# A decoder block on one core: 208 instead of 192 tokens take the gathered path of the expert layer, with other buffers and another order of its routing

## The chip, the cores and the metric

The kernel runs on one core of one Trainium2 chip. The metric is the time of one execution on the device in microseconds (us). The kernel before took 3613.26 us (median of three runs, 3609.4 to 3621.5).

## The reference, cut to what matters

512 tokens of width 2048, all in float32. A norm and one projection give the inputs of two mixers, a short convolution and a stick-breaking attention; both are gated, summed, projected and added to x. Then comes the expert layer:

```
q      = xn @ wq                                # 8 heads x 2 x 128
scores = q . subkeys                            # two lists of 128 a head
top 16 of each list; 256 sums; top 16 of them   # 16 of 16384 experts a head
gate   = softmax(the 16 scores)
hidden = xn . u[idx]                            # 8 x 16 = 128 experts a token
out    = sum(gelu(hidden) * gate * v[idx])
x      = rmsnorm(x + out)
```

u and v have 16384 rows of 2048. Each token uses 128 of them.

## The kernel before, in words

**Two ways through the expert layer.** The first G0 = 192 tokens are *gathered*: for each of a token's 128 experts the row of u, and later of v, is fetched from memory. One round fetches one row for each of 128 partitions (an indirect transfer of 1 MB issued by POOL, L690); VectorE (DVE) multiplies it with the token's xn and sums (L701, table u), or adds it, scaled, to a sum (L708, table v). A tile of 128 tokens takes 128 rounds of u and 128 of v. The next 64 tokens lie twice in the 128 partitions, with half of the slots each, and take 64 + 64. At the end of a tile `finish` folds the copies, and `finish_rows` takes the last norm and stores. The other ND = 320 tokens go the *dense* way (`dense`): all 16384 experts are computed for them and multiplied by a matrix of gates that is zero nearly everywhere.

**Weights.** `whalf` loads 128x1024 numbers (0.5 MB) by an SP transfer into a raw tile, and `split` makes two float32r parts: ScalarE (ACT) writes whi (L130), DVE writes wlo (L131). `mm3` does three matmuls with them (L161 to L163), whose moving operand is the tokens: 256 columns in the mixers and queries, 320 in the dense stage. There are WHL = 3 pairs whi/wlo, and 4 raw tiles `wraw`. In the dense stage every second half goes to one of three `spare` tiles instead.

**Stages.** First token half: mixer, output projection, queries (until about 805 us). Second half: mixer (`ahead`, to 1480), output projection, queries (to 1706). Then `dense`: eight chunks of `up` (u products, 8 units each), then per chunk `down` (v products), and from the ninth chunk on `up` and `down` in turn. A unit is two halves of weights, 48 matmuls; the dense stage has 256.

**What runs beside.** Two generators are advanced by hand between the units. `side` is routing: per tile of 128 tokens the top 16 lists (`top16`), the sums, one-hot selections, and the indices and gates; later `gates` turns the gates of the dense tokens into planes, in NB = 20 blocks of 16 tokens, four groups each. Every yield of it names a cost, and `background` grants 1.0 to 1.25 a call. `gat` is the gather; `pump(rate)` grants rounds per unit (1.35, then 0.85 and 0.8; 1.0 in the second queries and early dense stage; behind the routing the rest is spread evenly, at 0.9 of the even rate in the first eight chunks). A fetch also waits for an anchor, an instruction two units back (`LAG`), and a row is consumed one round after its fetch (`DEPTH`); L701 and L708 keep their program order. The tile framework then orders each engine's instructions by a simulated timeline, so loads are often issued earlier than they stand in the program. The `row` tiles are four, shared by the gather, the attention and the loads of rows.

Of the kernel before, what the change touches and what calls it, by code (L numbers as in the profile page):

```python
# [18 lines left out]
P = 128  # L19
# [6 lines left out]
H = 8  # L26
# [5 lines left out]
NG2 = 64  # L32
# [30 lines left out]
SPB2 = 3  # L63
# [13 lines left out]
AHEAD = 8  # L77


@with_exitstack  # L80
def block_kernel(ctx, tc, a, out, dbg=None):
# [104 lines left out]
    def rms_scale(pool, x):  # L186
        ss = pool.tile([P, 2], F32, name="ss", bufs=2)
        for c in range(2):
            junk = ztile()
            nc.scalar.activation(junk, x[:, c * 1024:c * 1024 + 1024], AF.Square, accum_out=ss[:, c:c + 1])  # L190
        return rms_inv(ss)

    def rms_inv(ss):
        nc.vector.tensor_tensor(ss[:, 0:1], ss[:, 0:1], ss[:, 1:2], OP.add)
        nc.scalar.activation(ss[:, 0:1], ss[:, 0:1], AF.Sqrt, scale=1.0 / D, bias=epst)
        nc.vector.reciprocal(ss[:, 0:1], ss[:, 0:1])
        return ss[:, 0:1]
# [356 lines left out]
    def route(pool, tile_no, st):  # L554

        ls = pool.tile([P, 2, 8, 2, 16], F32, name="ls", bufs=1)
        tv, ti = ls[:, 0], ls[:, 1].bitcast(U32)
        for _ in range(8):
            while not st["topk"][tile_no]:
                yield "wait"  # L560
            for _ in range(2):
                src, g = st["topk"][tile_no].pop(0)
                tmp = pool.tile([P, P], F32, name="ttmp", bufs=2)
                top16(tmp, src, tv[:, g // 2, g % 2], ti[:, g // 2, g % 2])
            yield 2.0
        tif = pool.tile([P, 8, 2, 16], F32, name="tif", bufs=1)
# [3 lines left out]
        cand = spare()[:, 0:512].rearrange("p (h c) -> p h c", h=8)  # L570
        c0 = 0
        for a0, na, nb in GROUPS:
            nc.vector.tensor_tensor(cand[:, :, c0:c0 + na * nb].rearrange("p h (a b) -> p h a b", b=nb),
                                    tv[:, :, 0, a0:a0 + na].unsqueeze(3).broadcast_to([P, 8, na, nb]),
                                    tv[:, :, 1, 0:nb].unsqueeze(2).broadcast_to([P, 8, na, nb]), OP.add)
            c0 += na * nb
        yield 0.9
        sv = pool.tile([P, 8, 16], F32, name="sv", bufs=1)
        pos = pool.tile([P, 8, 16], U32, name="pos", bufs=1)
        for h in range(H):  # L580
            tmp = pool.tile([P, P], F32, name="ttmp", bufs=2)
            top16(tmp[:, 0:64], cand[:, h], sv[:, h], pos[:, h])
            if h % 2:
                yield 1.4
        eg = pool.tile([P, 3, 8, 16], F32, name="eg", bufs=2)

        ic = pool.tile([P, 2, 8, 16], U32, name="ic", bufs=1)
# [3 lines left out]
        fa = pool.tile([P, 8, 16], F32, name="fa", bufs=1)  # L591
        fb = pool.tile([P, 8, 16], F32, name="fb", bufs=1)
        f1 = pool.tile([P, 8, 16], F32, name="f1", bufs=1)
        f2 = pool.tile([P, 8, 16], F32, name="f2", bufs=1)
# [13 lines left out]
        yield 2.6  # L608
        for s, ab in enumerate((fa, fb)):
            for h in range(0, H, 4):  # L610
                oh = spare().rearrange("p (h s k) -> p h s k", h=4, s=16)
                nc.vector.tensor_tensor(oh, ab[:, h:h + 4].unsqueeze(3).broadcast_to([P, 4, 16, 16]),
                                        iota[:, 0:16].unsqueeze(1).unsqueeze(1).broadcast_to([P, 4, 16, 16]), OP.is_equal)
                nc.vector.tensor_tensor(oh, oh, tif[:, h:h + 4, s].unsqueeze(2).broadcast_to([P, 4, 16, 16]), OP.mult)
                nc.vector.tensor_reduce(eg[:, s, h:h + 4], oh, AX.X, OP.add)
                yield 3.5
        gate = eg[:, 2]
        nc.vector.tensor_tensor(gate, sv, sv[:, :, 0:1].broadcast_to([P, 8, 16]), OP.subtract)
        nc.scalar.activation(gate, gate, AF.Exp)
        gs = pool.tile([P, 8], F32, name="gs", bufs=1)  # L620
        nc.vector.tensor_reduce(gs, gate, AX.X, OP.add)
        nc.vector.reciprocal(gs, gs)
        nc.vector.tensor_tensor(gate, gate, gs.unsqueeze(2).broadcast_to([P, 8, 16]), OP.mult)
        flat = eg.rearrange("p s a b -> p s (a b)")
        idx = None
        if tile_no * P < G0:
            ef = pool.tile([P, P], F32, name="fa", bufs=1)
            nc.vector.scalar_tensor_tensor(ef, flat[:, 0], 128.0, flat[:, 1], OP.mult, OP.add)
            idx = late[1].tile([P, P], I32, name="idx", bufs=2)
            nc.vector.tensor_copy(idx, ef)  # L630
            if tile_no == 0:
                st["gate"] = late[1].tile([P, P], F32, name="gate", bufs=1)
                nc.vector.tensor_copy(st["gate"], flat[:, 2])
        if dbg:
            nc.sync.dma_start(dbg["eg"][tile_no], flat)
        st["routes"][tile_no] = idx, flat
        yield 1.2
# [43 lines left out]
    def gather_tile(pool, np_, nslot, idx, gate, load_x, load_acc, finish):  # L681
# [6 lines left out]
        def fetch(tab, s):  # L688
            g = row()[0:np_]
            ins = nc.gpsimd.indirect_dma_start(out=g, out_offset=None, in_=tab, in_offset=bass.IndirectOffsetOnAxis(ap=idx[0:np_, s:s + 1], axis=0))  # L690
# [4 lines left out]
        acc = None  # L695

        def consume(tab, s, g):
            nonlocal acc
# [4 lines left out]
            if s == 0:  # L703
                nc.scalar.activation(act[:, :nslot], hid[:, :nslot], AF.Gelu)
                nc.vector.tensor_tensor(act[:, :nslot], act[:, :nslot], gate[0:np_], OP.mult)
                acc = row()
                load_acc(acc)
            pin(nc.vector.scalar_tensor_tensor(acc[0:np_], g, act[:, s:s + 1], acc[0:np_], OP.mult, OP.add))  # L708

        ready = []  # L710
        for tab in ("u", "v"):
            for s in range(nslot):
                ready.append((tab, s, fetch(a[tab], s)))
                if len(ready) > DEPTH:
                    consume(*ready.pop(0))
                yield
        while ready:
            consume(*ready.pop(0))
            yield
        finish(acc)  # L720
# [12 lines left out]
    def gather(routes):  # L733
        idx = routes[0][0]
        yield from gather_tile(
            late[1], P, P, idx, st["gate"],
            lambda t: nc.sync.dma_start(t, xn2d[0:P]),
            lambda t: nc.sync.dma_start(t, x2d[0:P]),
            lambda t: finish_rows(t, slice(0, P), final_gain()))
        if not NG2:  # L740
            return
        S = P // (P // NG2)
        idx, eg = routes[1]
        idx2 = late[1].tile([P, S], I32, name="idx2")
        gate2 = late[1].tile([P, S], F32, name="gate2")
        for r in range(P // NG2):
            ps_, ss = slice(r * NG2, r * NG2 + NG2), slice(r * S, r * S + S)
            nc.sync.dma_start(idx2[ps_], idx[0:NG2, ss])
            nc.sync.dma_start(gate2[ps_], eg[0:NG2, 2, ss])

        def load_x(t):
            for r in range(P // NG2):
                nc.sync.dma_start(t[r * NG2:r * NG2 + NG2], xn2d[P:G0])

        def load_acc(t):
            nc.vector.memset(t, 0.0)
            nc.sync.dma_start(t[0:NG2], x2d[P:G0])

        def finish(t):
            for r in range(1, P // NG2):  # L760
                o = row()
                nc.sync.dma_start(o[0:NG2], t[r * NG2:r * NG2 + NG2])
                nc.vector.tensor_tensor(t[0:NG2], t[0:NG2], o[0:NG2], OP.add)
            finish_rows(t, slice(P, G0), final_gain())

        yield from gather_tile(late[1], P // NG2 * NG2, S, idx2, gate2, load_x, load_acc, finish)

# [136 lines left out]
    st = {"routes": [None] * 4}  # L904
# [4 lines left out]
    rounds = 2 * P + (2 * (P // (P // NG2)) if NG2 else 0)  # L909
# [9 lines left out]
    def routing(h):  # L919
        for tt in range(2):  # L920
            yield from route(rts[0], 2 * h + tt, st)
# [43 lines left out]
    def background(what, rate):  # L965
# [3 lines left out]
        due = min(due, 0.0) + (SIDE_A0 if not st["routes"][0] else SIDE_A if unit < GATES_AT else SIDE_G)  # L969
# [11 lines left out]
        if st["routes"][0] and what != "half":  # L981
# [115 lines left out]
```

## Time and profile before

| | |
|---|---|
| median of three runs | 3613.26 us |
| the profiled execution | 3619.12 us, span 3617.4 us |
| granted TensorE clock, mean | 0.992 |
| PE, PEld busy | 3513.1 us (97%), 3410.4 us (94%) |
| DVE, ACT, POOL busy | 2831.2 us (78%), 1616.3 us (45%), 659.3 us (18%) |
| moved by DMA | 1049.29 MB, of which indirect 402.68 MB |
| rounds of the gather | 192 of u, 192 of v |

PE is TensorE's matmuls, PEld its weight loads, which overlap them. The clock is a share of full speed. A wait is named "who line <- whom", with its sum, its count and the longest. The chain is the work that ended last, followed back from the end.

### The profile page before, as it was taken

Reading aid. Unit: us, or ns where it says so; the run is one execution under the profiler, and the core shown is the slowest. Engines: PE = TensorE matmul, PEld = TensorE weight load, DVE = VectorE, ACT = ScalarE, POOL = GpSimd, SP = SyncE. Lnnn points to the kernel's source line nnn. Section 1 sums busy time; section 2 is a strip of 40 time slices with the busy share of each in tenths; the row PEclk is TensorE's granted clock in tenths of the full one; section 3 lists DMA queues with packets and bytes.
Section 4 is the critical chain, followed back from the end, with each engine's and each line's share of the span. In section 5 each row is a group of like instructions: output and inputs, shape, how many; then the busy total and the mean of one; then the engine's idle time right before and its main releaser. Section 6 shows DMA issues by size and latency. Waiting matters only on the chain.

```text
span 3617.4 us, 63262 instructions
## 1 busy us (share of the span) xinstructions
PE 3513.1 (97%) x25347; PEld 3410.4 (94%) x25347; DVE 2831.2 (78%) x4022; ACT 1616.3 (45%) x2275; POOL 659.3 (18%) x520
## 2 busy tenths in 40 slices
PE   9999999999999999889999999999999999999998
PEld 8999998898888999779999999999999999999998
DVE  6565557559987878788999886888887878888886
ACT  6454445445555534544337773333333333333334
POOL 0000000001233322112131111221122322322220
PEclk9999999999999999999999999999999999999999
DMA  6556555654788889898888889899988988899884
GB/s 204 180 178 225 187 187 196 208 184 137 260 348 309 335 332 346 322 331 335 298 327 319 311 315 365 329 356 338 339 328 328 346 330 333 327 346 343 328 329 162
DMA packets 292920, 1049.29 MB, mean 290 GB/s; under 512 B 35921, under 2 KB 105169, under 8 KB 238673
## 3 DMA queue, kind: packets, MB, share of 16 engines
q1 hardware_dynamic: 237328, 642.56, 50.5%
q0 software_dynamic: 55296, 402.68, 28.7%
q8 instruction: 199, 3.26, 0.4%
q14 instruction: 97, 0.79, 0.1%
HBM read 996.57 MB, written 47.97 MB: 289 GB/s over the span
## 4 chain that ended last, share of the span: by engine, by line
PE 59%; DMA 5%; DVE 4%; issue 2%; ACT 1%; POOL 0%; SPq 0%; ACTq 0%; DVEq 0%; POOLq 0%
PE pj L163 10%; PE pj L161 10%; PE pj L162 10%; PE z L161 9%; PE z L162 9%; PE z L163 9%; DVE wlo L131 2%; DMA wraw<-in_w_in 2%; PE pj L673 2%; DMA row<-in_u,idx 1%; DVE row L701 1%; ACT whi L130 1%; PE z L439 1%; DMA row<-in_v,idx 0%; DMA wraw<-in_w_mix 0%
## 5 line engine op out<-in xcount | busy, mean ns | idle before, releaser
L130 ACT ACTIVATE whi<-wraw 128x1024 fp32r<-128x1024 f32 x827 | 874.1, 1059 | 1258.0 <-PE pj L162 723.2
L131 DVE TENSOR_TENSOR wlo<-wraw,whi 128x1024 fp32r<-128x1024 f32 x827 | 1008.3, 1223 | 412.5 <-ACT whi L130 405.6
L161 PE MATMUL pj<-xhi,whi 128*128 128x256 f32 x2560 | 723.5, 283 | 12.5 <-ACT whi L130 10.3
L163 PE MATMUL pj<-xhi,wlo 128*128 128x256 f32 x2560 | 720.4, 283 | 13.5 <-DVE wlo L131 13.4
L162 PE MATMUL pj<-xlo,whi 128*128 128x256 f32 x2560 | 718.1, 281 | 0.0
L161 PE MATMUL pj<-dxhi,whi 128*128 128x320 f32 (+1 forms) x2304 | 710.0, 308 | 4.5 <-ACT whi L130 4.3
L163 PE MATMUL pj<-dxhi,wlo 128*128 128x320 f32 (+1 forms) x2304 | 703.6, 307 | 3.4 <-DVE wlo L131 3.3
L162 PE MATMUL pj<-dxlo,whi 128*128 128x320 f32 (+1 forms) x2304 | 705.2, 306 | 0.0
L161 PE MATMUL z<-ahi,whi 128*128 128x320 f32 x2048 | 632.0, 310 | 3.9 <-ACT z L190 2.9
L162 PE MATMUL z<-alo,whi 128*128 128x320 f32 x2048 | 631.8, 309 | 2.4 <-DVE alo L131 2.4
L163 PE MATMUL z<-ahi,wlo 128*128 128x320 f32 x2048 | 630.6, 309 | 1.8 <-DVE wlo L131 1.8
L163 PEld LDWEIGHTS pj<-xhi,wlo 128*128 128x128 f32 x2560 | 481.6, 189 | 23.6 <-DVE wlo L131 20.9
L161 PEld LDWEIGHTS pj<-xhi,whi 128*128 128x128 f32 x2560 | 482.5, 188 | 21.1 <-ACT whi L130 14.4
L690 POOL DMA_INDIRECT row<-in_v,idx x192 | 292.7, 1525 | 1060.2 <-DVE row L708 429.8
L162 PEld LDWEIGHTS pj<-xlo,whi 128*128 128x128 f32 x2560 | 482.3, 188 | 2.8 <-issue 1.6
L708 DVE SCALAR_TENSOR_TENSOR row<-row,gact 128x2048 f32<-128x2048 f32 x192 | 450.3, 2345 | 27.2 <-DMA row<-in_v,idx 27.2
L701 DVE SCALAR_TENSOR_TENSOR row<-row,gx 128x2048 f32<-128x2048 f32 x192 | 438.3, 2286 | 31.2 <-DMA row<-in_u,idx 31.1
L690 POOL DMA_INDIRECT row<-in_u,idx x192 | 289.0, 1505 | 863.1 <-DVE row L701 239.9
L161 PEld LDWEIGHTS pj<-dxhi,whi 128*128 128x128 f32 x2304 | 434.3, 189 | 5.5 <-ACT whi L130 5.1
L163 PEld LDWEIGHTS pj<-dxhi,wlo 128*128 128x128 f32 x2304 | 432.9, 188 | 5.4 <-DVE wlo L131 5.4
L162 PEld LDWEIGHTS pj<-dxlo,whi 128*128 128x128 f32 x2304 | 434.0, 188 | 0.0
L130 ACT ACTIVATE whi<-spare 128x1024 fp32r<-128x1024 f32 x197 | 208.8, 1060 | 425.4 <-PE z L162 266.9
(232 smaller groups left out, 4979.8 us busy)
## 6 DMA issues: line engine op xcount, KB each, us to landing
wraw<-in_w_in SPq DMA_DIRECT2D x320, 512.0 KB
wraw<-in_uT SPq DMA_DIRECT2D x187, 512.0 KB
wraw<-in_vT SPq DMA_DIRECT2D x128, 512.0 KB
spare<-in_vT SPq DMA_DIRECT2D x128, 512.0 KB
spare<-in_uT SPq DMA_DIRECT2D x69, 512.0 KB
wraw<-in_w_mix SPq DMA_DIRECT2D x64, 512.0 KB
wraw<-in_w_out SPq DMA_DIRECT2D x64, 512.0 KB
wraw<-in_wq SPq DMA_DIRECT2D x64, 512.0 KB
```

What stands on the lines that cost most here:

```text
L130: nc.scalar.activation(hi, src, AF.Copy)
L131: nc.vector.tensor_tensor(lo, src, hi.bitcast(F32), OP.subtract)
L161: nc.tensor.matmul(acc, shi, mhi, start=first, stop=False)
L162: nc.tensor.matmul(acc, shi, mlo, start=False, stop=False)
L163: pe_last[0] = nc.tensor.matmul(acc, slo, mhi, start=False, stop=last)
L439: nc.tensor.matmul(z[:, c], stat.bitcast(F32), src[:, c], start=False, stop=True, skip_group_check=True)
L673: behind(nc.tensor.matmul(gp[:, t * P:t * P + P], oh[:, t, 0], oh[:, t, 1], start=True, stop=True))
L690: ins = nc.gpsimd.indirect_dma_start(out=g, out_offset=None, in_=tab, in_offset=bass.IndirectOffsetOnAxis(ap=idx[0:np_, s:s + 1], axis=0))
L701: pin(nc.vector.scalar_tensor_tensor(g, g, 1.0, gx, OP.mult, OP.mult, accum_out=hid[:, s:s + 1]))
L708: pin(nc.vector.scalar_tensor_tensor(acc[0:np_], g, act[:, s:s + 1], acc[0:np_], OP.mult, OP.add))
```

## The change

Before, tile 0 (128 tokens) and 64 tokens of tile 1 are gathered. Now a list of segments does it: 128 tokens, 64 (two copies), and 16 (eight copies, folded three times). 208 + 208 rounds. The dense stage keeps 304 tokens (19 gate blocks).

In the dense stage there is one `spare` tile, used by every fifth half, and a fourth whi/wlo pair, used by every fourth. The routing works on half a tile's heads at a time. The first four heads of tile 0 are done as soon as their scores exist, and the gather starts on their indices; tile 1's lists are made between, and the rest of its routing follows with all costs times four (`LATE_W`). The v sum goes into gx, the tile that held xn; x2d is loaded and added at the end of a segment. The square sums of `rms_scale` go through a small tile of SBUF, 256 columns at a time.

```diff
+SEGS = ((0, 0, 128), (1, 0, 64), (1, 64, 16))
-NG2 = 64
+NG2 = 80
-SPB2 = 3
+SPB2 = 1
+LATE_W = 4.0
 def whalf(src):
-        if spare_ok[0] and turns[0] % 2:
+        if spare_ok[0] and turns[0] % 5 == 0:
             raw = spare()
...
-        hi = wp.tile([P, 1024], F32R, name="whi", bufs=WHL)
-        lo = wp.tile([P, 1024], F32R, name="wlo", bufs=WHL)
+        if spare_ok[0] and turns[0] % (WHL + 1) == 0:
+            hi, lo = (late[2].tile([P, 1024], F32R, name=n, bufs=1) for n in ("whi4", "wlo4"))
+        else:
+            hi, lo = (wp.tile([P, 1024], F32R, name=n, bufs=WHL) for n in ("whi", "wlo"))
 def rms_scale(pool, x):
-        for c in range(2):
-            junk = ztile()
+        for c in range(8):
+            junk = pool.tile([P, 256], F32, name="junk", bufs=1)
...
 def route_lists(pool, tile_no, hh, st):          # new: lists of heads 4*hh to 4*hh+3
 def route(pool, tile_no, hh, st, w):             # the rest for these heads, costs times w
...
+            idx = late[1].tile([P, 64], I32, name=f"idx_{hh}", bufs=2)
+            nc.vector.tensor_copy(idx, ef)
+            st["idx"][tile_no].append(idx)
 def gather_tile(...):
...
-                acc = row()
-                load_acc(acc)
-            pin(nc.vector.scalar_tensor_tensor(acc[0:np_], g, act[:, s:s + 1], acc[0:np_], OP.mult, OP.add))
+                pin(nc.vector.tensor_scalar(gx, g, act[:, 0:1], None, OP.mult))
+                return
+            pin(nc.vector.scalar_tensor_tensor(g if s == nslot - 1 else gx, g, act[:, s:s + 1], gx, OP.mult, OP.add))
...
+                while s // idx[0].shape[1] >= len(idx):
+                    yield
 def gather(routes):
+        for tile_no, p0, n in SEGS:
...
+            def finish(t):
+                m = P // 2
+                while m >= n:
+                    o = row()
+                    nc.sync.dma_start(o[0:m], t[m:2 * m])
+                    nc.vector.tensor_tensor(t[0:m], t[0:m], o[0:m], OP.add)
+                    m //= 2
+                o = row()
+                nc.sync.dma_start(o[0:n], x2d[rows])
+                nc.vector.tensor_tensor(t[0:n], t[0:n], o[0:n], OP.add)
+                finish_rows(t, rows, final_gain())
 def routing(h):
-        for tt in range(2):
-            yield from route(rts[0], 2 * h + tt, st)
+        for hh in range(2):
+            yield from route_lists(rts[0], ta, hh, st)
+            yield from route(rts[0], ta, hh, st, 1.0)
+            if h:
+                yield from route_lists(rts[0], tb, hh, st)
+                yield from route(rts[0], tb, hh, st, 1.0)
+            else:
+                yield from route_lists(rts[0], tb, hh, st)
+                kept.append(st["ls"][tb])
+        for hh, ls in enumerate(kept):
+            st["ls"][tb] = ls
+            yield from route(rts[0], tb, hh, st, LATE_W)
 def background(what, rate):
-        due = min(due, 0.0) + (SIDE_A0 if not st["routes"][0] else SIDE_A if unit < GATES_AT else SIDE_G)
+        due = min(due, 0.0) + (SIDE_A0 if not st["idx"][0] else SIDE_A if unit < GATES_AT else SIDE_G)
...
-        if st["routes"][0] and what != "half":
+        if st["idx"][0] and what != "half":
```

## Rows read from the trace of the kernel before

**Rows 1.** The page: the span, and PE's busy time.

```profile
span 3617.4 us, 63262 instructions
PE 3513.1 (97%) x25347; PEld 3410.4 (94%) x25347; DVE 2831.2 (78%) x4022; ACT 1616.3 (45%) x2275; POOL 659.3 (18%) x520
```

**Rows 2.** Windows: length; PE, PEld, DVE, ACT, POOL busy; clock; DMA; GB/s.

```profile
740.00:805.00 65.00, 65.00 (x556) 65.00 (x555) 35.63 (x86) 26.80 (x33) 0.00 (x0) 1.00 0.52 172
805.00:905.00 100.00, 95.24 (x703) 84.12 (x701) 90.71 (x328) 55.08 (x65) 12.96 (x17) 1.00 0.43 142
905.00:1050.00 145.00, 136.70 (x1003) 121.21 (x1002) 133.73 (x249) 78.18 (x93) 49.87 (x45) 1.00 0.79 294
1050.00:1480.00 430.00, 399.03 (x3152) 378.10 (x3150) 341.70 (x376) 194.00 (x238) 116.01 (x92) 0.98 0.89 333
1706.00:2180.00 474.00, 468.70 (x3297) 465.88 (x3297) 426.55 (x966) 272.30 (x508) 85.74 (x58) 1.00 0.87 314
1800.00:1900.00 100.00, 99.38 (x676) 98.85 (x675) 98.40 (x197) 37.35 (x45) 29.12 (x13) 1.00 0.89 322
2215.00:2660.00 445.00, 439.82 (x2981) 436.93 (x2980) 381.57 (x365) 156.81 (x186) 89.71 (x63) 1.00 0.92 342
2400.00:2500.00 100.00, 99.08 (x673) 98.30 (x672) 86.88 (x85) 34.36 (x40) 21.71 (x16) 1.00 0.94 353
2660.00:3550.00 890.00, 887.11 (x6025) 886.16 (x6025) 725.98 (x657) 320.28 (x393) 228.39 (x140) 1.00 0.88 332
```

**Rows 3.** Windows with PE never idle, at 256 columns and at 320.

```profile
400.00:500.00 100.00, 100.00 (x851) 100.00 (x850) 57.72 (x72) 42.86 (x53) 0.00 (x0) 1.00 0.56 185
2860.00:3360.00 500.00, 500.00 (x3409) 499.75 (x3409) 411.39 (x382) 173.95 (x210) 140.61 (x83) 1.00 0.89 337
```

**Rows 4.** Timeline of ACT: start, duration, instruction, idle before and its releaser.

```profile
3001.84 1.06 ACT L130 ACTIVATE whi<-wraw 128x1024 fp32r<-128x1024 f32 x1 [2.46 <-PE z L162]
3005.36 1.06 ACT L130 ACTIVATE whi<-spare 128x1024 fp32r<-128x1024 f32 x1 [2.46 <-PE z L162]
```

**Rows 5.** Waits: span (four rows), DVE from 2260 to 3520, PE in 1000:1100.

```profile
POOL row L690 <- DVE row L708: 429.8, 88, 13.3
POOL row L690 <- DVE row L701: 247.2, 42, 25.3
DVE row L701 <- DMA row<-in_u,idx: 31.1, 24, 5.0
DVE hb L779 <- DMA gt<-gd: 8.7, 1, 8.7
...
DVE row L701 <- DMA row<-in_u,idx: 0.9, 2, 0.6
...
PE pj L163 <- DVE wlo L131: 6.7, 9, 1.2
```

**Rows 6.** Chain of waits: start, us, what; a gate group, a plane, a finish.

```profile
1499.85 0.89 PE pj L673 x8
...
2185.14 15.56 DMA gt<-gd
...
2747.74 1.16 ACT z L190 x2
```

**Rows 7.** Windows, columns as in rows 2: the plane's load, the first finish.

```profile
2180.00:2240.00 60.00, 56.14 (x364) 55.21 (x363) 37.23 (x38) 20.82 (x30) 11.37 (x7) 0.94 1.03 394
2740.00:2760.00 20.00, 17.14 (x99) 16.87 (x98) 14.63 (x15) 9.47 (x14) 2.77 (x2) 0.83 0.93 341
```

**Rows 8.** Windows of L690 alone (us, POOL busy); L701 and L753 by tile.

```profile
2180.00:2740.00 560.00, 114.02 (x79) 0.99 0.92 343
2740.00:3550.00 810.00, 210.95 (x128) 1.00 0.88 333
...
L701 DVE SCALAR_TENSOR_TENSOR row<-row,gx x192: 2241/2284/2486, 908.6 to 3147.6; 128x2048 f32<-128x2048 f32 x192
L753 SPq DMA_DIRECT2D gx<-xn2d x2: 480/534/588, 1797.2 to 1797.7; - x2
```

More of the change, by code (lines that the diff above doesn't have):

```diff
@@ L552, in top16, with route_lists @@
         nc.vector.max_index(ti[:, 8:16], tv[:, 8:16], tmp)
-    def route(pool, tile_no, st):
-        ls = pool.tile([P, 2, 8, 2, 16], F32, name="ls", bufs=1)
+    def route_lists(pool, tile_no, hh, st):
+        ls = st["ls"][tile_no] = pool.tile([P, 2, 4, 2, 16], F32, name="ls", bufs=3)
         tv, ti = ls[:, 0], ls[:, 1].bitcast(U32)
-        for _ in range(8):
+        for _ in range(4):
             while not st["topk"][tile_no]:
@@ L573, in route @@
             nc.vector.tensor_tensor(cand[:, :, c0:c0 + na * nb].rearrange("p h (a b) -> p h a b", b=nb),
-                                    tv[:, :, 0, a0:a0 + na].unsqueeze(3).broadcast_to([P, 8, na, nb]),
-                                    tv[:, :, 1, 0:nb].unsqueeze(2).broadcast_to([P, 8, na, nb]), OP.add)
+                                    tv[:, :, 0, a0:a0 + na].unsqueeze(3).broadcast_to([P, 4, na, nb]),
+                                    tv[:, :, 1, 0:nb].unsqueeze(2).broadcast_to([P, 4, na, nb]), OP.add)
             c0 += na * nb
[L577 to L580, printed above, removed]
+        yield 0.5 * w
+        sv = pool.tile([P, 4, 16], F32, name="sv", bufs=1)
+        pos = pool.tile([P, 4, 16], U32, name="pos", bufs=1)
+        for h in range(4):
             tmp = pool.tile([P, P], F32, name="ttmp", bufs=2)
@@ L607, in route @@
         nc.vector.tensor_tensor(fb, fb, f1, OP.add)
-        yield 2.6
+        yield 1.8 * w
         for s, ab in enumerate((fa, fb)):
[L610 to L616, printed above, removed]
@@ new lines, in route @@
+            nc.vector.tensor_reduce(eg[:, s, hs], oh, AX.X, OP.add)
+            yield 3.5 * w
+        flat = eg.rearrange("p s a b -> p s (a b)")
+        fs = slice(64 * hh, 64 * hh + 64)
+        if tile_no * P < G0:
+            ef = pool.tile([P, 64], F32, name="fa", bufs=1)
+            nc.vector.scalar_tensor_tensor(ef, flat[:, 0, fs], 128.0, flat[:, 1, fs], OP.mult, OP.add)
+            idx = late[1].tile([P, 64], I32, name=f"idx_{hh}", bufs=2)
+            nc.vector.tensor_copy(idx, ef)
+            st["idx"][tile_no].append(idx)
@@ L619, in route @@
+        gate = eg[:, 2, hs]
+        nc.vector.tensor_tensor(gate, sv, sv[:, :, 0:1].broadcast_to([P, 4, 16]), OP.subtract)
         nc.scalar.activation(gate, gate, AF.Exp)
-        gs = pool.tile([P, 8], F32, name="gs", bufs=1)
+        gs = pool.tile([P, 4], F32, name="gs", bufs=1)
         nc.vector.tensor_reduce(gs, gate, AX.X, OP.add)
         nc.vector.reciprocal(gs, gs)
-        nc.vector.tensor_tensor(gate, gate, gs.unsqueeze(2).broadcast_to([P, 8, 16]), OP.mult)
-        flat = eg.rearrange("p s a b -> p s (a b)")
@@ L636, in route @@
-        st["routes"][tile_no] = idx, flat
-        yield 1.2
+        nc.vector.tensor_tensor(gate, gate, gs.unsqueeze(2).broadcast_to([P, 4, 16]), OP.mult)
+        if tile_no == 0:
+            if hh == 0:
+                st["gate"] = late[1].tile([P, P], F32, name="gate", bufs=1)
+            nc.vector.tensor_copy(st["gate"][:, fs], flat[:, 2, fs])
+        if hh:
+            if dbg:
+                nc.sync.dma_start(dbg["eg"][tile_no], flat)
+            st["routes"][tile_no] = st["idx"][tile_no], flat
@@ L639, in gates @@
+        yield 1.2 * w
     def gates(pool, eg, p0, b0, nb):
@@ L679, in gates, with gather_tile @@
                 nc.sync.dma_start(gd[b0 + g // 4], stage)
-    def gather_tile(pool, np_, nslot, idx, gate, load_x, load_acc, finish):
+    def gather_tile(pool, np_, nslot, idx, gate, load_x, finish):
         gx = late[1].tile([P, D], F32, name="gx", bufs=1)[0:np_]
@@ L717, in gather_tile @@
         while ready:
+            g = ready[0][2]
             consume(*ready.pop(0))
             yield
-        finish(acc)
+        finish(g)
     def final_gain():
@@ L733, in gather @@
     def gather(routes):
[L734 to L760, printed above, removed]
+        for tile_no, p0, n in SEGS:
+            R = P // n
+            rows = slice(tile_no * P + p0, tile_no * P + p0 + n)
+            idx, gate = st["idx"][tile_no], st["gate"]
+            if R > 1:
+                src, eg = routes[tile_no]
+                idx = [late[1].tile([P, n], I32, name=f"idx{n}")]
+                gate = late[1].tile([P, n], F32, name=f"gate{n}")
+                for r in range(R):
+                    ps_, ss = slice(r * n, r * n + n), slice(r * n, r * n + n)
+                    c = r * n % 64
+                    nc.sync.dma_start(idx[0][ps_], src[r * n // 64][p0:p0 + n, c:c + n])
+                    nc.sync.dma_start(gate[ps_], eg[p0:p0 + n, 2, ss])
+            def load_x(t):
+                for r in range(R):
+                    nc.sync.dma_start(t[r * n:r * n + n], xn2d[rows])
+            def finish(t):
[5 more added lines that the diff above has]
+                    m //= 2
@@ L768, in dense @@
+            yield from gather_tile(late[1], P, n, idx, gate, load_x, finish)
     def dense(pool, st):
@@ L902, in dense @@
                 nc.sync.dma_start(out[G0 + c:G0 + c + n, half * 1024:half * 1024 + 1024], xs)
-    st = {"routes": [None] * 4}
+    st = {"routes": [None] * 4, "eg": [None] * 4, "idx": [[] for _ in range(4)], "ls": [None] * 4}
     credit = 0.0
@@ L908, in block_kernel @@
     pumped = [0]
-    rounds = 2 * P + (2 * (P // (P // NG2)) if NG2 else 0)
+    rounds = sum(2 * n for _, _, n in SEGS)
     def pump(rate):
```

62 lines of the change are left out of this document (30 added, 32 removed).

## The prediction

> **What bounds the kernel now.** I read the page first [rows 1]: PE is busy 3513.1 of 3617.4 us, so a change pays if it shortens TensorE's work and does not open new gaps in it. VectorE (78%) and the transfers are next. A mean says little here, so I cut the span into the kernel's stages [rows 2]: PE busy, DVE busy, granted clock, share of the DMA engines and GB/s stand side by side. The gathers run from 901 us on. Between 905 and 1480 us, the rest of the second half's mixer, PE stands idle 8.3 + 31.0 of 575 us (6.8%); behind it, in the dense stage, it idles 5.3 us up to 2180, 5.2 in 2215 to 2660 and 2.9 in 2660 to 3550. So the dense stage (1706 to 3605) is TensorE's, and there the DMA engines are 0.87 to 0.92 busy and DVE 0.82 to 0.90.
>
> I call 48 matmuls on 1 MB of weights a unit (two halves of 24); the dense stage has 256 units, 12288 matmuls of 320 columns. Then I took the pace: 3409 such matmuls in 500 us are 146.7 ns each, and 851 of 256 columns in 100 us are 117.5 ns [rows 3]; that is 0.456 ns a column. A unit takes 7.04 us. The splits show that nothing else sets this pace: ScalarE starts one each 3.52 us, every time after 2.46 us of waiting for PE [rows 4]. Last I read the waits of DVE and POOL [rows 5], the places where PE did stop [rows 6, 7], and the gathers' counts and durations [rows 8].
>
> **The change, part by part.**
>
> (1) 320 to 304 columns. 16 x 0.456 = 7.29 ns for each of 12288 matmuls: **-89.6 us**; strict proportion to columns would give -90.1. A unit comes to 6.69 us.
>
> (2) Gate blocks fall from 20 to 19: four groups of eight recorded matmuls at 0.89 us [rows 6]: **-3.6 us**.
>
> (3) The squares of a finished tile no longer go through a z tile of PSUM. At 2745 us ScalarE's two writes into z end PE's wait, and 2740 to 2760 holds 99 matmuls at clock 0.83 [rows 6, 7] where 20 us hold 136 at 146.7 ns; about 37 are missing, **-5.5 us**. PE's 2.9 us of idle time in 2660 to 3550 [rows 2] are these 2.86 alone, so the second finish, later, shows no such gap and it counts once.
>
> (4) Buffers. In the dense stage the raw ring goes from four and three alternating to five, the split pairs from three to four, so a half may be split three ahead of PE and not two, some 3.3 us more cover against a late DVE. Memory in flight stays at nine to ten halves. Where PE stops in 2180 to 2215 (DVE in order behind the gate plane's transfer, 15.56 us [rows 6]) that saves up to 7 us; I take **-1**. The sums of the v rows now go into gx, so a fetch finds four row buffers and not three: POOL waited 429.8 us for L708 against 247.2 for L701 [rows 5]. I cost that at nothing; POOL is idle most of the time.
>
> (5) Routing in the dense stage (tiles 2 and 3) and its gates. The work is the same, in halves of four heads, with some more short instructions (I count 3 us). DVE has 426.6 us to do in 474; with 20 us less it is 0.95 busy. Bounds: 0, since at 0.98 PE lost 0.6 of 100 us [rows 2], and +23 if 0.90 is what DVE can do. I take **+8**, between, because there is little slack to catch up before the gate planes are wanted.
>
> (6) Transfers. 32 more rounds of 1.05 MB. Counting the pumps in the loops: the gather now starts 13 units earlier at 1.35 rounds a unit, which takes 18 of them into 808 to 905 us; 14 are left for the stretch after the routing: 222 rounds in place of 208, +5% at 0.9 of the pace up to the end of the first eight chunks, +7% behind. Per unit 2215 to 2660 moves 342 x 7.04 = 2.41 MB and 2660 to 3550 332 x 7.04 = 2.34; with about one and 1.11 rounds a unit [rows 8], 5% smaller planes and the shorter unit, 2.44 MB and 2.41 MB in 6.69 us are 365 and 361 GB/s, at a DMA share of some 0.98 and 0.96. Bounds: 0, since 2180 to 2240 held 394 GB/s for 60 us [rows 7]; +66 us, the whole gain of these 190 units, if the engines give nothing over their present mean. I take **+9**, nearer to the first: from 2260 to 3520 DVE waited 0.9 us for u rows [rows 5].
> The Trainium skill speaks against this part ("DMA: Bandwidth & Descriptors", Where 436 GB/s comes from): between HBM and SBUF the HBM side binds, at about 358 GB/s a core. By it the two stretches would need, as an estimate, 6.83 and 6.74 us a unit, 15 us lost and not 9. The 394 GB/s of these 60 us do not agree with it as a hard limit.
>
> (7) Three finishes and two changes of tile. gx now holds the sum until the last v row, so the next tile's xn load cannot be issued in the v phase (now it goes out at 1797 us, right after the u phase [rows 8]); x2d is loaded and added at the end, and the 16 token tile folds three times through SBUF copies. DVE runs in order: an operation that waits for such a load holds up the wlo splits queued behind it, and PE's cover is three halves, 10 us. On SP the gx load waits for the last v row, and the weight loads queue behind it. Lower bound 0 (all covered), upper +25: three times the 8.7 us that DVE stood for the gate plane [rows 5]. I take **+8**. The last segment's chain runs beside the eight units of the last chunk, 54 us, so the end stays with the dense rows. Each finish puts eight squares of 256 columns on ScalarE, an estimate of 3 to 4 us from 1.06 us for 1024; three waits of 2.46 us cover them [rows 4].
>
> (8) Mixer and routing before 1480 us. Half of tile 0's routing moves into the query stage (DVE 35.6 of 65 us from 740 to 805 [rows 2]), tile 1's is spread over 58 units at a quarter of the density, and 905 to 1050 gets lighter (wlo stalls 6.7 us in 1000 to 1100 [rows 5]). Against that 805 to 905, DVE already 0.91, gets 18 rounds of 2.3 us on DVE [rows 8] and 180 GB/s. Bounds: -7, those wlo stalls gone; +5, if 805 to 905 loses what 100 us of 1050 to 1480 lose (7.2 us idle and 2% of clock) in place of its 4.8. I take **+4**: the rows are added, the routing on DVE is only moved.
>
> Sum: -89.6 -3.6 -5.5 -1 +8 +9 +8 +4 = -70.7 us. The profiled execution took 3619.1 us (span 3617.4), 5.9 over the median of 3613.3; the same step from the median gives **3542 us**. Its own range, with (5) to (8) at a half or double and the ends not together: 3515 to 3572.
>
> **Rivals.**
>
> A, slower: the transfers' present mean is their ceiling (342 and 332 GB/s). It is decided in 2215 to 3550, whose units then carry more bytes at the same rate: 2.44/342 and 2.41/332 are 7.15 and 7.27 us, so +36 us over 190 units in place of -66 + 9. Sum +22: 3635. It speaks for it that the DMA share is 0.92 and 0.88 and that the added rows are 33.6 MB; against it the 394 GB/s and a PE that never waits for a weight there. It makes the kernel slower if the ceiling lies below 341 GB/s (460 MB in 1348 us); 362 gives the full gain.
>
> B, no change: near 0.97 the gather rows come late, DVE stands in order before L701 or L708, and wlo comes late, as in 905 to 1480, where DMA shares are 0.79 to 0.89 and PE loses 6.8%. On 1269 us that is 86, less the 8 lost now: +78 and not +9. Sum -2: 3611. Against it: there a unit takes 5.6 us of PE and the attention shares the row buffers; for it: L701 waited 31.1 us in all for rows, all but 0.9 before 2260 us [rows 5].
>
> C, a smaller gain: bursts reach 394 GB/s, but a lasting load gets no more than the best 100 us do, 353 GB/s in 2400 to 2500 with PE 99.1 busy [rows 2]. Then 2.44/353 and 2.41/353 are 6.91 and 6.83 us a unit, 14 + 18 = 32 us lost in (6) and not 9. Sum -48: 3565, inside the forecast's own range. Against it: no stretch before asked for more than 353 for long. The Trainium skill's figure named under (6) is a rule of this kind; with it the sum would be -65.
>
> D, better: cover and buffers hide (5) to (8) entirely: -99.7, or 3514.
>
> **How the numbers follow.** Chances: forecast 0.57, C 0.17, D 0.10, B 0.08, A 0.08. What a measurement here can tell from no change is 0.3%, 11 us. Forecast, C and D are faster; of B one part in four is still faster, half the same, one part slower; A is slower by over 11 us in nearly all its cases. So faster 0.86, same 0.05, slower 0.09. The range: from 3512 (D and a little) to 3592 (where half of B's price is paid); A and most of B stay out.
>
> **What would show it.** 2860 to 3360 us: some 3580 matmuls in 500 us (139.4 ns) and splits 3.35 us apart; if it is fewer with DMA at 1.0, (6) is A or C; if DVE shows waits for rows, B. No gap in PE at the first finish, near unit 116; instead a look for DVE waiting on gx or row<-x2d there and near unit 221. The first gather near 810 us, PE idle in 805 to 905 at most some 4 us over now. Gate planes in time: PE busy over 98% up to the first vT block. Wrong altogether if the dense stage (1706 to 3605, 1899 us) is not at least 50 us shorter.

## The result, and the profile after

The changed kernel takes 3649.82 us (median of four runs, 3644.61 to 3657.08) against 3612.52 for the kernel before: a ratio of 1.0105 (95% interval 1.0081 to 1.013). It is slower, by 1%; forecast were 3542 us and a dense stage shorter by at least 50 us. The profiled execution took 3650.53 us.

The page of the kernel after:

```profile
span 3648.8 us, 63430 instructions
PE 3461.6 (95%) x25315; PEld 3348.8 (92%) x25315; DVE 2900.8 (79%) x4164; ACT 1628.7 (45%) x2313; POOL 720.1 (20%) x552
```

TensorE has 51.5 us less to do than in [rows 1], and the span is 31.4 us longer: 82.9 us more of it are not busy. The busy time fell by 51.5 us and not by the 99 of the first three steps, and the granted clock from 0.992 to 0.983: a part of the matmuls has become longer than its columns ask for.

Two markers split the span. The first gelu of the dense stage (tile hd, ACT) ends its first unit; the first gate product (hd by gt, DVE) stands behind the first eight chunks, at about unit 128. Tile hd, before and after; the last columns are ns (least, median, most), first and last start in us, and form:

```profile
L803 ACT ACTIVATE hd<-pj x128: 413/418/438, 1714.5 to 3541.7; 128x320 f32<-128x320 f32 x128
L779 DVE TENSOR_TENSOR hd<-hd,gt x64: 478/484/493, 2698.9 to 3542.2; 128x320 f32<-128x320 f32 x64
```

```profile
L825 ACT ACTIVATE hd<-pj x128: 398/423/427, 1752.1 to 3572.3; 128x304 f32<-128x304 f32 x128
L801 DVE TENSOR_TENSOR hd<-hd,gt x64: 456/470/477, 2739.3 to 3573.6; 128x304 f32<-128x304 f32 x64
```

Up to the first marker the kernel loses 37.6 us; between them it takes 987.2 us in place of 984.4; from the second to the end 909.5 in place of 918.5. At 0.35 us less a unit (7.04 to 6.69) both dense parts should have been about 45 us shorter before any loss. Windows of after, columns as in [rows 2]:

```profile
740.00:805.00 65.00, 65.00 (x557) 65.00 (x556) 52.23 (x200) 28.75 (x37) 0.00 (x0) 1.00 0.51 171
805.00:905.00 100.00, 92.48 (x684) 83.55 (x684) 94.98 (x272) 56.11 (x66) 22.41 (x24) 0.98 0.69 246
905.00:1050.00 145.00, 130.84 (x929) 116.78 (x929) 134.29 (x262) 66.08 (x79) 50.61 (x45) 0.96 0.79 295
1706.00:2180.00 474.00, 460.69 (x3382) 456.70 (x3381) 439.50 (x1016) 270.04 (x490) 84.44 (x61) 0.99 0.87 317
2215.00:2660.00 445.00, 420.25 (x2914) 415.64 (x2913) 370.30 (x359) 155.90 (x204) 122.58 (x63) 0.98 0.94 347
2660.00:3400.00 740.00, 709.47 (x4990) 703.18 (x4988) 613.12 (x563) 257.42 (x321) 207.97 (x127) 0.99 0.91 345
2660.00:3550.00 890.00, 855.81 (x6013) 848.48 (x6012) 747.90 (x691) 316.57 (x398) 254.81 (x157) 0.99 0.92 349
2860.00:3360.00 500.00, 488.88 (x3456) 485.66 (x3455) 422.72 (x373) 177.73 (x222) 144.75 (x90) 0.99 0.92 352
```

The row to read first is 2860 to 3360: 3456 matmuls, where 3409 ran before at 320 columns [rows 3] and 3580 were forecast. PE, never idle there before, now idles 11.1 us. In 2215 to 2660 it idles 24.8 us in place of 5.2, and in 2660 to 3550 34.2 in place of 2.9. The matmuls have become shorter and start hardly any closer together.

What PE waits for in 2215 to 3550, and what stands behind it (rows of PE, DVE, ACT and SP; sum in us, count, longest):

```profile
PE z L168 <- DVE wlo L134: 39.5, 27, 5.0
...
DVE wlo L134 <- ACT whi L133: 55.3, 44, 12.6
...
ACT whi L133 <- DMA wraw<-in_vT: 153.0, 56, 14.3
...
SPq L148 <- DVE wlo L134: 860.3, 306, 11.5
```

Read it from the bottom: SP may load a raw half when DVE has split the one that lay there; the load lands late, so ScalarE's whi is late, so wlo is, and PE stands. The chain of after at the first finish shows such transfers (start, us, what); a wraw load is half a megabyte, a gate plane gt 1.2 MB:

```profile
2606.67 15.66 DMA gt<-gd
2622.39 14.63 DMA wraw<-in_vT
2637.04 20.77 DMA gx<-xn2d
...
2674.08 25.00 DMA wraw<-in_vT
```

### The profile page after: what moved, and what is told of

Its sections match the earlier page's. It is cut to its first block, busy times and chain, and to the rows that moved or that the text cites. A ratio compares the mean times of both kernels' runs of the same rounds, so it can differ in the third digit from the quotient of the medians.

```text
span 3648.8 us, 63430 instructions
## 1 busy us (share of the span) xinstructions
PE 3461.6 (95%) x25315; PEld 3348.8 (92%) x25315; DVE 2900.8 (79%) x4164; ACT 1628.7 (45%) x2313; POOL 720.1 (20%) x552
## 4 chain that ended last, share of the span: by engine, by line
PE 44%; issue 14%; DVE 10%; DMA 9%; POOL 3%; ACT 2%; SPq 0%; DVEq 0%; ACTq 0%; POOLq 0%
PE pj L168 9%; PE pj L166 9%; PE pj L167 9%; PE z L168 4%; PE z L167 4%; PE z L166 4%; POOL row L712 3%; DVE wlo L134 3%; DMA row<-in_u,idx 2%; DVE row L720 2%; DMA wraw<-in_vT 2%; PE pj L692 2%; DMA row<-in_v,idx 1%; DVE gx L727 1%; PE z L448 1%
## 5 line engine op out<-in xcount | busy, mean ns | idle before, releaser
L133 ACT ACTIVATE whi<-wraw 128x1024 fp32r<-128x1024 f32 x946 | 996.4, 1058 | 1300.3 <-PE pj L167 627.2
L134 DVE TENSOR_TENSOR wlo<-wraw,whi 128x1024 fp32r<-128x1024 f32 x946 | 1146.3, 1220 | 335.7 <-ACT whi L133 331.5
L166 PE MATMUL pj<-xhi,whi 128*128 128x256 f32 x2560 | 727.8, 285 | 16.8 <-ACT whi L133 11.1
L168 PE MATMUL pj<-dxhi,wlo 128*128 128x304 f32 (+1 forms) x2304 | 692.2, 302 | 12.0 <-DVE wlo L134 11.7
L166 PE MATMUL pj<-dxhi,whi 128*128 128x304 f32 (+1 forms) x2304 | 698.3, 304 | 4.0 <-ACT whi L133 3.0
L167 PE MATMUL pj<-dxlo,whi 128*128 128x304 f32 (+1 forms) x2304 | 694.1, 302 | 0.0
L168 PE MATMUL z<-ahi,wlo 128*128 128x304 f32 x2048 | 627.6, 308 | 39.6 <-DVE wlo L134 39.5
L166 PE MATMUL z<-ahi,whi 128*128 128x304 f32 x2048 | 625.7, 306 | 14.9 <-ACT whi L133 12.8
L167 PE MATMUL z<-alo,whi 128*128 128x304 f32 x2048 | 625.8, 306 | 0.0
L712 POOL DMA_INDIRECT row<-in_u,idx x208 | 300.9, 1447 | 1391.7 <-DVE ttmp L559 504.0
L712 POOL DMA_INDIRECT row<-in_v,idx x208 | 349.9, 1682 | 1025.2 <-DVE dacc L865 315.7
L727 DVE SCALAR_TENSOR_TENSOR gx<-row,gact,gx 128x2048 f32<-128x2048 f32 x202 | 473.5, 2344 | 11.9 <-DMA row<-in_v,idx 11.5
L168 PEld LDWEIGHTS z<-ahi,wlo 128*128 128x128 f32 x2048 | 391.4, 191 | 47.1 <-DVE wlo L134 46.9
```

What stands on the lines that cost most here:

```text
L133: nc.scalar.activation(hi, src, AF.Copy)
L134: nc.vector.tensor_tensor(lo, src, hi.bitcast(F32), OP.subtract)
L166: nc.tensor.matmul(acc, shi, mhi, start=first, stop=False)
L167: nc.tensor.matmul(acc, shi, mlo, start=False, stop=False)
L168: pe_last[0] = nc.tensor.matmul(acc, slo, mhi, start=False, stop=last)
L727: pin(nc.vector.scalar_tensor_tensor(g if s == nslot - 1 else gx, g, act[:, s:s + 1], gx, OP.mult, OP.add))
```

## The experiments

All are timed against the kernel before, as is after. They are called x1 to x6, z1 to z3 and d1 to d3, by the start of their labels.

**Do the new buffers or the sum in gx cost it?**

x1:

```diff
-SPB2 = 1
+SPB2 = 3
-        if spare_ok[0] and turns[0] % 5 == 0:
+        if spare_ok[0] and turns[0] % 2:
# and no fourth whi/wlo pair
```

> The changed kernel, but with the old rings: four wraw and three spare raw tiles in turn, three whi/wlo pairs. Theory P (three parts of the change cost separately: the smaller raw ring, the early start over the attention, the two changes of tile): ScalarE's waits for in_vT fall from 153 us to under 20, the first eight chunks' down stage loses some 25 us less than in the changed kernel, 3620 to 3630 us. Theory Q (the 32 added rounds fill the transfers and DVE, wherever the buffers are): 3645 to 3660 us, since a deeper ring gives no more bandwidth.

x2:

```diff
-                pin(nc.vector.tensor_scalar(gx, g, act[:, 0:1], None, OP.mult))
-                return
-            pin(nc.vector.scalar_tensor_tensor(g if s == nslot - 1 else gx, g, act[:, s:s + 1], gx, OP.mult, OP.add))
+                acc = row()
+                load_acc(acc)
+            pin(nc.vector.scalar_tensor_tensor(acc[0:np_], g, act[:, s:s + 1], acc[0:np_], OP.mult, OP.add))
# and no x2d load and add in finish
```

> The changed kernel, but the v rows are again summed in a row tile of their own that starts from x2d, so gx is free after the u phase and xn of the next segment is loaded early, and no x2d is added at the end. Theory P: the two changes of tile (near 2640 and 3370 us) lose some 20 us less, 3625 to 3635 us. Theory Q: 3645 to 3660 us, or slower, with one row tile less for the fetches.

Measured: old buffers 1.0124 (1.0105 to 1.0144), own sum 1.0126 (1.0093 to 1.016). Neither gives anything back. With the old buffers, over the whole span,

```profile
ACT whi L133 <- DMA wraw<-in_vT: 2.3, 1, 2.3
```

ScalarE's 153 us of waiting for wraw loads are gone, and no time is won: in 2215 to 3550 PE still waits 29.6 us for wlo in z (39.5 in after), and SP 915.9 us (860.3) for wlo to free a raw half. The wait is named at another place of the same ring. Its size is no price.

**Do the 16 tokens cost it, and does the early start?** x3:

```diff
-        if st["idx"][0] and what != "half":
+        if st["routes"][0] and what != "half":
```

> The changed kernel, but the gather starts only when the whole of tile 0 is routed (unit 16 of the second mixer, not unit 1); some 20 rounds move from there into the dense stage. Theory P: the 30 us lost between 912 and 1317 us come back at most by half, since the later rounds lie over the attention in either kernel, and the dense stage loses some 10: 3635 to 3650. Theory Q: the dense stage has 20 more rounds to carry and gets slower by 20 to 50 us: 3660 to 3690.

x4:

```diff
-SEGS = ((0, 0, 128), (1, 0, 64), (1, 64, 16))
+SEGS = ((0, 0, 128), (1, 0, 64))
```

> The changed kernel without its last segment: 16 of the 208 gathered tokens are computed nowhere, 384 rounds in place of 416, the dense stage at 304 tokens. Theory Q: with the old number of rounds the dense stage gains what the narrower matmuls give: under 3570 us. Theory P: only the third finish and 8% of the rounds go; the ring, the early start and one change of tile stay: 3610 to 3630 us.

Late start: 1.0106 (1.008 to 1.0132), as after. Without the third segment (its 16 tokens are computed nowhere): 0.9927 (0.991 to 0.9943), so 32 rounds and their finish cost some 64 us (1.0105 less 0.9927), 2 us a round, and a round holds DVE for 2.3 [rows 8]. Tile hd of the late start:

```profile
L825 ACT ACTIVATE hd<-pj x128: 399/423/427, 1706.9 to 3560.8; 128x304 f32<-128x304 f32 x128
L801 DVE TENSOR_TENSOR hd<-hd,gt x64: 462/476/516, 2693.4 to 3561.3; 128x304 f32<-128x304 f32 x64
```

The dense stage begins 45.2 us earlier than in after, and in the profiled runs 34.2 of them are lost again behind it: 943.7 us from the second marker to the end, not 909.5. This profiled run is the fastest of its four (3638.93 us); by the medians nothing is left of the 45. Before the first marker after issues 138 rounds and this kernel 116: 45.2 us over 22 rounds is about the same 2 us a round. While the dense stage cannot carry them free, little is won by where they stand.

**VectorE or bytes?** Three kernels do the 416 rounds at half cost; only their time is meant.

```diff
# d1: half of each row multiplied and added, all of it fetched
-    pin(nc.vector.scalar_tensor_tensor(g, g, 1.0, gx, OP.mult, OP.mult, accum_out=hid[:, s:s + 1]))
+    pin(nc.vector.scalar_tensor_tensor(g[:, 0:1024], g[:, 0:1024], 1.0, gx[:, 0:1024], OP.mult, OP.mult, accum_out=hid[:, s:s + 1]))
# ... and the same for the sums of the v rows
# d2: half of each row fetched, and used twice
-    ins = nc.gpsimd.indirect_dma_start(out=g, out_offset=None, in_=tab, ...
+    ins = nc.gpsimd.indirect_dma_start(out=g[:, 0:1024], out_offset=None, in_=tab.rearrange("e (a d) -> (e a) d", a=2), ...
# ... and DVE works on it in two instructions of 1024 columns, as much as before
# d3: both
```

> The changed kernel with all 416 rounds and all their bytes, but VectorE works on 1024 of a row's 2048 columns only (half of each product and sum is left out, but for the first v row of a segment). Theory V (a round costs its 2.3 us on VectorE, whose in-order queue makes the splits late): 1.1 us less for each of 416 rounds; the mixer's and the dense stage's losses go and the time falls under 3580 us. Theory T (a round costs its 1.05 MB, since the transfers give some 350 GB/s and no more under a lasting load): 3630 to 3655 us, PE in 2660 to 3460 still at 96% with the rate at 345 to 355 GB/s.

> The changed kernel with all 416 rounds, but each fetches half a row (0.5 MB), and VectorE uses that half twice, so that its work stays (two instructions of 1024 columns; a wrong half of the table's rows is read). Theory T: DMA falls from 0.92 to about 0.75 in the dense stage, PE is over 99% busy there, and the time is under 3570 us. Theory V: VectorE's work is the same or a little more, the time stays at 3640 to 3670 us.

> The changed kernel with 416 rounds that fetch half a row and work on that half only (half of each product and sum is left out). If VectorE's time and the bytes are all that the rounds cost, nothing is left but TensorE's own pace and the stops seen before the change: 3525 to 3550. If the two changes of tile, the gate planes or the order of the instructions cost more beside: over 3560.

Half of DVE's work: 0.9889 (0.9875 to 0.9903). Half of the bytes: 0.9968 (0.9954 to 0.9983). Both: 0.9731 (0.9714 to 0.9749). By stage, in us of the profiled runs:

| | to the first marker | between | second to end | span |
|---|---|---|---|---|
| before | 1714.5 | 984.4 | 918.5 | 3617.4 |
| after | 1752.1 | 987.2 | 909.5 | 3648.8 |
| half DVE work | 1715.7 | 951.3 | 904.0 | 3571.0 |
| half bytes | 1758.2 | 965.5 | 878.6 | 3602.3 |
| both | 1712.8 | 929.4 | 876.8 | 3519.0 |

The two effects very nearly add up. Ahead of the dense stage it is DVE alone (36 to 45 us; bytes nothing). Between the markers both count: DVE 36, bytes 22. Behind, it is bytes (31 and 27) and hardly DVE (2 to 6). The waits agree: in 2215 to 3550 ScalarE still waits 142.4 us for in_vT with half the DVE work, and PE's waits for wlo in z go from 39.5 to 25.6 us with half the DVE work, and with half the bytes they are gone. Windows of 2215 to 2660 and 2660 to 3400, first half DVE work, then half bytes, then both:

```profile
2215.00:2660.00 445.00, 426.52 (x2975) 422.22 (x2974) 322.37 (x383) 158.02 (x198) 98.23 (x68) 0.98 0.95 352
2660.00:3400.00 740.00, 724.69 (x5106) 722.19 (x5105) 492.67 (x577) 266.31 (x343) 181.33 (x133) 0.99 0.93 354
```

```profile
2215.00:2660.00 445.00, 427.53 (x3000) 425.94 (x2999) 390.93 (x439) 164.56 (x213) 118.41 (x65) 0.98 0.82 282
2660.00:3400.00 740.00, 737.10 (x5249) 736.36 (x5249) 658.01 (x800) 277.19 (x347) 221.67 (x136) 1.00 0.79 269
```

```profile
2215.00:2660.00 445.00, 439.56 (x3139) 437.94 (x3138) 333.07 (x398) 170.33 (x211) 130.69 (x72) 1.00 0.83 288
2660.00:3400.00 740.00, 738.55 (x5285) 738.30 (x5284) 517.50 (x592) 281.74 (x350) 196.44 (x137) 1.00 0.78 271
```

Count matmuls in 2660 to 3400: 4990 after, 5106, 5249, 5285. With a lighter DVE the transfers go to 354 GB/s, PE still idle 15 us; with lighter transfers DVE can be 0.89 busy and PE loses 3 us, and in 2860 to 3360 it runs the forecast 3580 matmuls without a stop. With both halved the span is 98.4 us below that of before, the 98.7 of the first three steps. The halving lightens all 416 rounds, not the 32 new ones alone, so this is no proof of what a fix would give, and that the two numbers meet is partly luck.

**What is each layer of the change worth?**

```diff
# x6: the edits of x4 and x3 together (304 columns, 384 rounds, late start)
# z1: x6, and 320 columns and the squares in a z tile as before
-NG2 = 80
+NG2 = 64
-        for c in range(8):
-            junk = pool.tile([P, 256], F32, name="junk", bufs=1)
+        for c in range(2):
+            junk = ztile()
# z2: z1 and the edit of x1
# z3: x3, and more rounds in the second half's mixer
-RATE_A2 = 0.85
-RATE_O = 0.8
+RATE_A2 = 1.05
+RATE_O = 1.0
# x5: after, tile 1's late routing not spread
-LATE_W = 4.0
+LATE_W = 1.0
```

> The changed kernel without its last segment (16 tokens computed nowhere) and with the gather starting only after all of tile 0 is routed: both costs taken away at once. If a round costs the same 2.2 us wherever it is added (from 3585 us without the segment, the 20 early rounds only move into the dense stage): 3580 to 3590. If the early start is a cost of its own, over the attention, and the dense stage has room for 20 rounds more at 384 in all: 3540 to 3560.

> 192 gathered and 320 dense tokens as before, and the gather starting when tile 0 is routed, as before; what stays of the change is the routing by half tiles, the v sum in gx, five raw tiles and four split pairs (and, for want of SBUF, the squares go through a z tile again). If all that these parts do is done before the dense stage (in the changed kernel with the late start the mixer ended 13 to 19 us earlier than before): 3592 to 3604 us. If the new rings cost something in the first eight chunks at 320 columns too: 3605 to 3620.

> As the run before, with the old rings (four and three raw tiles, three split pairs). If the rings matter little at this load, within 6 us of it; if the weights' late arrivals at five raw tiles cost time, 8 to 15 us less: 3585 to 3600.

> 208 tokens with the late start, and the pump rates 0.85 and 0.8 of the later mixer and the output projection at 1.05 and 1.0, so some 15 rounds move out of the dense stage into 1170 to 1600 us. If a round costs the same anywhere: 3638 to 3656, as without the move. If it costs less where VectorE is 0.8 busy and the weights need fewer bytes a us than the dense stage's planes and rows together: 3610 to 3635.

> The changed kernel with the costs of tile 1's late routing at their plain size (1 and not 4), so it is no longer spread in program order. If the spreading acts on the chip, as the prediction had it, the routing falls back on 905 to 1050 us and the kernel gets slower by 5 to 10 us. If the framework's order undoes it (in the changed kernel tile 1's last indices were ready at 1056 us, 300 us before their place in program order), within 8 us of the changed kernel: 3642 to 3658.

Measured: x6 0.9859 (0.9845 to 0.9873), z1 1.0042 (1.0028 to 1.0055), z2 1.0034 (1.0021 to 1.0046), z3 1.0117 (1.0101 to 1.0133), x5 1.0138 (1.012 to 1.0155). Outside both times that were written down for them lie x4 (3584.8 us), half bytes (3600.6), both halves (3519.2), x5 (3662.3) and z1 (3627.9); x6 (3560.4) lies at the edge of one, and x3 (3646.7) inside one that had foreseen smaller shifts than its 45 and 34 us. The ratios make a ladder, in us of 3612.5 (x4 and x6 leave 16 tokens out):

| step | ratio | us |
|---|---|---|
| before to z1: order, buffers, sum in gx, late x2d | 1.0042 | +15 |
| z1 to x6: 304 columns, one gate block less, no squares in PSUM | 0.9859 | -66 |
| x6 to x3: the last 16 tokens, 32 rounds | 1.0106 | +89 |
| x3 to after: early start | 1.0105 | 0 |

z2 shows that the buffers are not the 15 us. z3 moves rounds into the mixer and changes nothing, as an equal price in both places says.

The first two steps do not part the change cleanly. z1's squares go through z again, and its two finishes meet PE worse than those of before. Its tile hd, and what PE waited for, in z1 and in before:

```profile
L824 ACT ACTIVATE hd<-pj x128: 409/422/441, 1713.4 to 3541.9; 128x320 f32<-128x320 f32 x128
L800 DVE TENSOR_TENSOR hd<-hd,gt x64: 480/490/495, 2693.5 to 3543.2; 128x320 f32<-128x320 f32 x64
PE z L166 <- ACT z L195: 10.3, 2, 6.0
...
PE z L161 <- ACT z L190: 2.9, 1, 2.9
```

In the profiled runs z1 is 1.1 us shorter than before up to the first marker and 4.3 between the markers; it loses 14.2 behind the second, where its finishes are. PE waits 10.3 us there for the squares, 16.0 in z2. The changed kernel has no squares in z. So at least 7 of the 15 us are no cost that it carries, and they stand as a gain in the step to x6, of which some 59 us are then left for the narrower matmuls and the gate block.

With 192 tokens gathered, where the dense stage has some room, the early start does cost: x4 is 24 us slower than x6.

## Why the prediction was wrong

**(1) to (3), -98.7.** The cost of a column was right: the row with both halved runs 5285 matmuls in 740 us, 140.0 ns, and 139.4 were forecast. But z1 to x6, with 384 rounds beside, gave 66 us and not 99. Between the markers, where neither has a finish, x6 is 32.0 us shorter than z1, not 45:

```profile
L825 ACT ACTIVATE hd<-pj x128: 393/407/427, 1712.6 to 3487.5; 128x304 f32<-128x304 f32 x128
L801 DVE TENSOR_TENSOR hd<-hd,gt x64: 457/471/477, 2660.7 to 3490.9; 128x304 f32<-128x304 f32 x64
```

In 2215 to 2660 and 2660 to 3400 x6 moves 349 GB/s, and PE idles 11.5 and 16.6 us: a shorter unit brings even the old rows near the limit. Of (3), the two writes into z no longer end a wait of PE, yet PE does not run through the first finish: 2600 to 2700 holds

```profile
2600.00:2700.00 100.00, 89.51 (x618) 87.69 (x617) 77.74 (x81) 35.81 (x54) 27.50 (x15) 0.98 0.99 361
```

10.5 us idle, while gt, wraw and gx queue on full transfers (the chain above).

**(4) -1.** About right as a sum: with the old buffers the ratio stays inside the interval of the new ones, at 416 rounds (x1 and after) and at 384 (z2 and z1). The cover of a third half bought nothing while loads were late.

**(5) +8 and (7) +8.** With (4) they were given +15, and z1, which has all of them but the third segment's share, shows +15. That is luck: z1 loses nothing up to unit 128, where (5) was priced, and at least 7 of its 15 us are its squares in z. At 416 rounds (5) cannot be told from the rows that stand beside it: DVE was 0.93 busy in 1706 to 2180 and halving its work there and up to unit 128 gave 36 us. Of (7) DVE's wait for gx was small (one row, below), and x2, which takes the sum out of gx, wins nothing.

```profile
DVE row L720 <- DMA gx<-xn2d: 3.5, 1, 3.5
```

One claim of (7) was wrong: the end did not stay with the dense rows. From the last gate product to the end there are 75.2 us before and after, though the last eight units are 2.8 us shorter, and without the third segment 71.1. The chain of after ends through it:

```profile
3574.94 2.36 DVE row L727
3577.32 4.21 DMA row<-row
...
3583.94 2.99 DMA row<-row
...
3589.97 4.35 DMA row<-x2d
...
3599.38 6.94 DMA row<-x2d
```

Against the kernel without the third segment that is some 4 us, inside the step's bounds.

**(6) +9: the step that failed.** The bytes were counted well: 144 rounds between the second marker and 3550 us where 134 stood before, 8% more. What failed is the price, taken near zero because 60 us had held 394 GB/s and because DVE hardly waited for rows. The stretches that needed 365 and 361 GB/s got 347 and 349 (2215 to 2660, 2660 to 3550), with half the DVE work 352 and 354 (the second up to 3400), in the late start 349 and

```profile
2660.00:3500.00 840.00, 790.91 (x5506) 782.71 (x5505) 709.27 (x645) 293.20 (x383) 257.38 (x154) 0.98 0.93 356
```

The highest 100 us of after hold

```profile
3400.00:3500.00 100.00, 96.34 (x665) 95.30 (x666) 88.54 (x92) 40.53 (x54) 31.10 (x21) 0.98 0.97 375
```

so bursts exist, but no stretch of 445 us that was looked at passes 360 (late start, 2660 to 3105). The sign that the prediction named for such a ceiling, a DMA share of 1.0, did not come: PE stood with the share at 0.91 to 0.95. That DVE did not wait for rows was the wrong waiter to look at: what came late in PE's chain were the weights. The step was also priced by bytes alone. Each round also puts 2.3 us on DVE, which stood at 0.82 to 0.90 in the dense stage [rows 2], ahead of wlo splits; up to unit 128 that counts for more than the bytes, behind it hardly. The ladder's +89 for 32 rounds, 2.8 us a round, is (6) with the third finish of (7); the kernels with half the cost of all 416 rounds put 47 to 52 us on bytes and 78 to 83 on DVE, by which is halved first.

**(8) +4: mis-sized as well, +37.6.** PE's idle time in a like window was taken as the upper bound, while the sum that decides was DVE's: 90.7 us in 805 to 905 [rows 2], plus 18 rounds of 2.3 (41), less the 16.6 moved into 740 to 805 (35.6 to 52.2), are 115 us in 100. The trace does not bear this out as it stands: up to 905 only 11 rounds were fetched (L712: us, POOL busy),

```profile
700.00:905.00 205.00, 13.81 (x11) 0.98 0.64 218
```

and DVE, with 22.9 us of them, went to 0.95. 805 to 905 lost 2.8 us of PE, as allowed, 905 to 1050 another 5.9 and 4% of clock. The two hold 93 matmuls less than before, some 11 us at 117.5 ns; the rest of the 37.6 is lost later in the mixer and the queries. The 18 rounds did come, but over the whole stage: 138 up to the first marker where 120 stood, again about 2 us each. With half of DVE's work on the rows 36.4 us come back, all behind 1050 us (the two windows stay at 91.0 and 129.1 us of PE); with half the bytes none. So DVE's time on the rows is shown as the cause for the stage, but not for one window of it. Nor did the routing spread: the last indices of tile 1 are ready at the same time in after and with LATE_W at 1 (tile idx of each):

```profile
L639 DVE CAST idx<-fa x4: 171/181/184, 817.1 to 1055.7; 128x64 int32<-128x64 f32 x4
```

```profile
L639 DVE CAST idx<-fa x4: 181/184/196, 819.1 to 1057.4; 128x64 int32<-128x64 f32 x4
```

In the total this step costs nothing against a late start, since the 22 rounds come dear there too.

**The rivals.** A comes nearest: 3635, with a price where it put it, in 2215 to 3550. But its sum is right partly by luck: its ceiling was a little low (342 and 332 GB/s; 347 to 356 measured), so that from the first marker on it forecast 18 us more than before where 6.2 less were measured, and ahead of it it had +4 for 37.6. C had the better ceiling, 353, and was the smaller loss because it charged bytes alone. B's signature, DVE standing for late rows, is not there: in 2215 to 3550 its L727 waited 6.2 us for v rows. D's sum appears only with the rounds halved. The Trainium skill ("DMA: Bandwidth & Descriptors", Where 436 GB/s comes from) puts some 358 GB/s between HBM and SBUF for a core. As a limit on long stretches the runs agree within 1% (at most 360 over 445 us, 356 over 840); over 60 to 100 us they show 394 and 375. By that figure alone the sum would still have been -65, so it was no warning. The prediction's own range was also narrower below than said: with (5) to (8) at a half the sum gives 3528, not 3515, which is nearly D.

**Open.** Whether the ceiling lies in the DMA engines (share 0.91 to 0.95 in those windows) or behind them; why x5 is 12 us slower than after with the same tile 1 times; what, beside the squares in z, makes z1's 15 us; and how much of the halves' gain belongs to the 384 old rounds. A version faster than before with all tokens computed was not found.

## What to carry to other kernels

When work moves from a bound engine to engines that look 80 to 90% busy, price it on each of them by summing the stage's busy time with the addition, in order, before asking which wait ends last; here a round that held DVE for 2.3 us made the span 2.0 (x4 to after) to 2.8 us (x6 to x3) longer, in stages where DVE or the transfers were about 0.9 busy. And a test kernel that puts back one part of the old code (here the squares in z) adds that part's cost to its step: look for its wait in the trace before you read a price from the ladder. Take the bandwidth that a stage can ask for from its longest busy stretch, not from its best 60 us, and look for lateness at every transfer that TensorE's chain waits for (here the weights), not only at the one that was added. A saving per unit is worth its full size only if everything else that runs per unit shrinks too.

## What was not expected of the hardware

A stretch with short stops of TensorE can lose clock too. 1000 to 1100 us, after and then before:

```profile
1000.00:1100.00 100.00, 85.57 (x586) 75.83 (x586) 77.19 (x107) 49.18 (x57) 27.91 (x31) 0.93 0.69 259
```

```profile
1000.00:1100.00 100.00, 91.19 (x661) 80.37 (x661) 88.72 (x99) 52.64 (x61) 40.26 (x34) 1.00 0.89 345
```

In after the granted clock is 0.93, a mean over times at 2.4 and at 1.2 GHz, and PE stood idle for 14.4 us in pieces; before, 8.8 us of stops cost none. In 2215 to 2660 of after it is 0.98, and 2914 matmuls take 420.25 busy us where 139.6 ns each (500 us over 3580, half bytes) would be 406.8. So of the 38 us by which that stretch falls short of its pace, 25 are idle and 13 slower or later matmuls.

A load of 0.5 MB, of which one is needed every 3.35 us, took 14.63 and 25.00 us of the chain beside a gate plane and rows. At most nine halves, 30 us, lie between the start of a load and PE's use of it (five raw tiles, four split pairs), and fewer when DVE is behind.
